# Another order for the 32 experts of a mixture-of-experts stage, and 64-row gathers for its half blocks

## The chip, the cores and the metric

The kernel runs on one core of one Trainium2 chip. The metric is the device time of one execution in microseconds (us); of several runs the median counts. Engines are named as in the profile: PE is TensorE (PEld its weight loads), DVE is VectorE, ACT is ScalarE, POOL is GpSimd, SP is SyncE, which here issues the large loads.

## The reference

One decoder layer with 2048 tokens of width 1024 in float32: projections, an RWKV-7 mixer and a dilated attention, an output product with layer norm, and then the part that the change touches, a mixture of 32 experts (two for each token), added to a gated embedding term, with a last layer norm. The expert part, cut:

```python
eid = grp[:, None] * EXPERTS_PER_GROUP + top_i          # two experts for each token
...
def run_block(args):                                    # 128 rows of one expert
    xblk, e = args
    hdn = jax.nn.silu(xblk @ w_gate[e]) * (xblk @ w_up[e])
    return hdn @ w_down[e]
...
return jnp.zeros((N, D), x2.dtype).at[row_tok].add((yb * row_w[:, None]).astype(x2.dtype))
```

`w_gate` and `w_up` are 1024 x 512 for each expert and `w_down` is 512 x 1024, so an expert has 6.3 MB of weights whatever the number of its tokens.

## The kernel before

The layer runs in stages: project, mixers, mix_out, route, ple (the gated embedding), experts, finish. The change touches the experts stage.

**Sizes and order.** The experts are sorted on the chip by how many tokens they got. `RANKS` (line 35) holds, for each place in that sorting, a size in units of 64 rows: one expert of 7, one of 5, one of 4, ten of 3, thirteen of 2 and six of 1. An expert of size n has n // 2 full blocks of 128 rows and, where n is odd, one half block of 64. `_order` (lines 39 to 48) fixes in which order the ranks are worked: it picks at each step the rank that keeps the sum of `UNITS` closest to its mean. `ORDER` and `CAPS` (sizes in that order) come from it. Before the change `CAPS` is 2,3 eight times, and then 2,2,3,2,3,2,4,2,1,5,1,1,1,7,1,1. Below, "a 3" is an expert of size 3.

**Groups.** `experts_begin` cuts each expert into groups of at most two blocks (line 1654). A 2 or a 1 is one group of one block; a 3 is one group of a full and a half block, a 4 one group of two full blocks; a 5 is a group of two full blocks and a group of one half block; a 7 is a group of two full blocks and one of a full and a half block.

**Work of a block.** float32 values are split into a high part (`copy` to fp32r on ACT) and a low part (subtraction on DVE), and a product is a sum of products of parts. A full block takes three matmuls of 512 columns for each 128 rows of weights (lines 198 to 200, `mm3`). A half block lays the high and low parts of its 64 rows beside each other in one operand and takes two (lines 1755, 1756); its two row halves have to be added afterwards (`sums`, lines 1768, 1769, and lines 1836, 1837). For each block the stage runs: `turn` (4+4 transposes of the gathered rows `xg` on PE, line 1746, then the parts `XX` on ACT and DVE, lines 1748, 1749), `pe_gate` (16 or 24 matmuls, then silu into `hd` on ACT, line 1789), `pe_up` (as many, then `hd` times it on DVE, line 1804), `pe_turn` (four transposes of `hd`, line 1812, then `HX` on ACT and DVE, lines 1813, 1814), `pe_down` (16 or 24 matmuls, then `ysb`), and a scatter that adds `ysb` to the result rows (line 1840, on POOL's queue).

**Weights.** Each expert has 12 pieces of 512 KB. SP loads them into 8 buffers (`raw`, `fetch`, line 1659), and `split` (line 1705) makes `wh` on ACT (line 1710) and `wl` on DVE (line 1711), two instructions of 512 columns each, into 12 buffers. `need` (line 1715) issues the splits at most six pieces (`LEAD`) ahead of the product.

**Order on the engines.** PE and ACT run in the order of the code; for the other engines a scheduler chooses. How a group of one block is joined to the next group matters below:

```python
more = turn(i + 1)
along(pe_up(i, 0), more)
...                                       # a group of two blocks does its products here, and pe_gate(i + 1) last
    along(pe_gate(i + 1), nothing, 3, lambda: pe_turn(i, 0))
run(pe_down(i, 0))
```

So after a one-block group PE runs the first three quarters of the next group's gate product, then the four transposes of `hd`, then the last quarter of that gate product, and then the down product, which needs `HX`.

**Gathers.** `gather(i)` (lines 1675 to 1680) fetches the rows of a group's blocks by an indirect DMA on POOL's queue, two groups ahead, into two buffers `xg`, always 128 rows; rows past the count of a block go to rows that are not used. `ix`, `sl` and `wd` are tables of row numbers and weights, loaded by POOL (lines 1641 to 1649) over the range of places that have such a block.

Of the kernel before, what the change touches and what calls it, by code (L numbers as in the profile page):

```python
# [18 lines left out]
P = 128  # L19
# [7 lines left out]
NE = 32  # L27
# [7 lines left out]
RANKS = (7, 5, 4) + (3,) * 10 + (2,) * 13 + (1,) * 6  # L35
UNITS = {n: n // 2 * 3 + n % 2 * 2 for n in range(33)}


def _order():

    left, done, order = list(range(NE)), 0, []
    mean = sum(UNITS[RANKS[r]] for r in left) / NE
    for n in range(NE):
        r = min(left, key=lambda r: (abs(done + UNITS[RANKS[r]] - AHEAD - mean * (n + 1)), r))
        left.remove(r)
        order.append(r)
        done += UNITS[RANKS[r]]
    return tuple(order)


AHEAD = 0.0
ORDER = _order()
CAPS = tuple(RANKS[r] for r in ORDER)
NW, NR, NX, NXX, NHX, NHD = 12, 8, 2, 4, 2, 2
# [113 lines left out]
class K:  # L168
# [1462 lines left out]
    def experts_begin(self):  # L1631

        nc, tc, I = self.nc, self.tc, self.I
        cp, rp = self.early
        lists = self.slots_[0:NE * CAP].rearrange("(e b p) w -> p e b w", b=CAP // P, p=P)
        nblk = (max(CAPS) + 1) // 2
        sl = cp.tile([P, NE, nblk, 2], F32, name="sl")
        ix = cp.tile([P, NE, nblk], I32, name="ix")
        wd = cp.tile([P, NE, nblk], F32, name="wd")
        for b in range(nblk):  # L1640
            js = [e for e in range(NE) if CAPS[e] > 2 * b]
            lo, hi = min(js), max(js) + 1
            nc.gpsimd.dma_start(sl[:, lo:hi, b], lists[:, lo:hi, b])
            nc.gpsimd.tensor_copy(ix[:, lo:hi, b], sl[:, lo:hi, b, 0])
            js = [e for e in range(NE) if CAPS[e] == 2 * b + 1]
            if js:
                lo, hi = min(js), max(js) + 1
                for h in range(2):
                    nc.gpsimd.dma_start(wd[h * 64:(h + 1) * 64, lo:hi, b:b + 1], lists[0:64, lo:hi, b, 1:2])
        self.lists = sl, ix, wd  # L1650
        groups = []
        for e in range(NE):
            blocks = [(e, b, CAPS[e] == 2 * b + 1) for b in range((CAPS[e] + 1) // 2)]
            groups += [(e, blocks[j:j + 2], j + 2 >= len(blocks)) for j in range(0, len(blocks), 2)]

        self.groups = groups
        self.raws, self.xgs, issued = {}, {}, []

        def fetch(g):

            e, n = divmod(g, NCH)
            if n == 0:
                at = tc.issue_after(issued[-NCH].ins) if len(issued) >= NCH else ExitStack()
                with at:
                    self.who = nc.values_load(self.ord[0:1, e:e + 1], engines=[mybir.EngineType.SP], min_val=0, max_val=NE - 1)
            self.raws[g] = raw = rp.tile([P, D], F32, name="raw5", tag="raw5")
            if n < 8:
                src = I["w_gate" if n < 4 else "w_up"][0].rearrange("e (k p) f -> p (e k) f", p=P)
                ins = nc.sync.dma_start(raw.rearrange("p (k f) -> p k f", k=2), src[:, bass.ds(self.who * KC + n % 4 * 2, 2)])
            else:  # L1670
                src = I["w_down"][0].rearrange("e d f -> (e d) f")
                ins = nc.sync.dma_start(raw, src[bass.ds(self.who * DE + (n - 8) * P, P)])
            issued.append(ins)

        def gather(i):
            if i >= len(groups):
                return
            for e, b, half in groups[i][1]:
                self.xgs[e, b] = xg = cp.tile([P, D], F32, name="xg", tag="xg", bufs=NX)
                nc.gpsimd.indirect_dma_start(out=xg, out_offset=None, in_=self.x2, in_offset=bass.IndirectOffsetOnAxis(ap=ix[:, e, b:b + 1], axis=0))  # L1680

        self.fetch, self.gather = fetch, gather
        self.ln2 = [self.rows_to(cp, n, I[n][0]) for n in ("ln2_g", "ln2_b")]
        for g in range(NR):
            fetch(g)
        gather(0)

    def experts(self):
# [307 lines left out]
```

## Time and profile before

| | us |
|---|---|
| median of 3 runs | 3246.5 (3241.99 to 3250.48) |
| profiled execution, its own time | 3253.92 |
| span of the profiled execution | 3252.1 |
| of it the expert products on PE, 2315.7 to 3171.5 | 855.8 |
| PE busy over the span | 2928.5 (90%) |
| DVE, ACT, POOL busy | 2113.1, 1526.9, 675.3 |

The profile is one execution taken by the hardware profiler. A busy PE is modelled from pipelined matmuls. In a line of the trace's timeline, the bracket at the end is how long the engine stood idle before the instruction, and what released it. The granted clock of PE is a share of 2.4 GHz.

### The profile page before, as it was taken

What the parts mean: (1) busy time and instruction counts of PE and PEld (TensorE: products, weight loads), DVE (VectorE), ACT (ScalarE), POOL (GpSimd) and SP (SyncE); (2) the same over time, 40 slices, a digit from 0 to 9 for tenths busy, and PEclk for the clock granted to TensorE, in tenths of its full rate; (3) what the DMA queues carried; (4) which work ended last, traced back from release to release, by engine and by line L of the source; (5) the groups of instructions that cost most, each with busy time, mean ns of one, the idle gap of its engine ahead of it and who ended that gap; (6) DMA issues with size and microseconds to landing.
All of it is one profiled execution on the core that took longest, in us unless ns stands there. A gap on an engine that the chain in (4) does not pass through costs nothing. (4 is left out here: it accounts for less than half of the span.)

```text
span 3252.1 us, 49914 instructions
## 1 busy us (share of the span) xinstructions
PE 2928.5 (90%) x17038; PEld 2335.2 (72%) x17039; DVE 2113.1 (65%) x4730; ACT 1526.9 (47%) x3650; POOL 675.3 (21%) x682
## 2 busy tenths in 40 slices
PE   8989888999798998998997899899999999998880
PEld 6666777777687777777786677788777777776560
DVE  4997333686564755666657678653587787766756
ACT  3444211555454544544444233311477777765642
POOL 0442000244100312112102122223011111112216
PEclk9999989999799889988898899999999999999885
DMA  5212433688725335235205453243499999987845
GB/s 166 80 56 95 103 88 80 203 273 266 154 60 123 100 79 132 69 76 139 65 22 144 138 177 123 96 140 94 175 307 323 324 304 322 313 295 225 289 130 210
DMA packets 364064, 533.09 MB, mean 164 GB/s; under 512 B 92376, under 2 KB 204640, under 8 KB 363792
## 3 DMA queue, kind: packets, MB, share of 16 engines
q1 hardware_dynamic: 330144, 459.09, 44.4%
q0 software_dynamic: 14496, 45.93, 6.0%
q10 hardware_dynamic: 19168, 24.86, 3.1%
q8 instruction: 136, 2.23, 0.3%
q14 instruction: 120, 0.98, 0.1%
HBM read 402.27 MB, written 128.06 MB: 163 GB/s over the span
## 5 line engine op out<-in xcount | busy, mean ns | idle before, releaser
L1711 DVE TENSOR_TENSOR wl<-raw,wh 128x512 fp32r<-128x512 f32 x768 | 478.0, 681 | 88.5 <-ACT wh L1710 87.9
L1710 ACT CAST wh<-raw 128x512 fp32r<-128x512 f32 x768 | 417.5, 620 | 12.2 <-DMA raw<-in_w_up_dram 10.5
L198 PE MATMUL ps<-xh,wh 128*128 128x512 f32 x640 | 263.1, 411 | 0.3 <-ACT xh L322 0.3
L199 PE MATMUL ps<-xl,wh 128*128 128x512 f32 x640 | 259.2, 405 | 0.9 <-DVE xl L323 0.8
L200 PE MATMUL ps<-xh,wl 128*128 128x512 f32 x640 | 257.9, 403 | 0.0
L1088 ACT ACTIVATE pe<-pe,ms 128x256 f32<-128x256 f32 (+1 forms) x384 | 174.9, 457 | 161.0 <-DVE ms L1085 153.3
L1840 POOL DMA_INDIRECT acc<-ysb,ix x48 | 96.5, 2010 | 623.0 <-ACT ysb L1839 402.6
L198 PE MATMUL pe<-wh,XX 128*128 128x512 f32 x480 | 199.3, 415 | 3.8 <-ACT wh L1710 3.8
L199 PE MATMUL pe<-wl,XX 128*128 128x512 f32 x480 | 191.8, 400 | 2.6 <-DVE wl L1711 2.6
L200 PE MATMUL pe<-wh,XX 128*128 128x512 f32 x480 | 190.7, 397 | 0.0
L198 PEld LDWEIGHTS ps<-xh,wh 128*128 128x128 f32 x640 | 125.1, 195 | 34.2 <-issue 2.8
L199 PEld LDWEIGHTS ps<-xl,wh 128*128 128x128 f32 x640 | 124.7, 195 | 29.9 <-DVE xl L323 2.3
L200 PEld LDWEIGHTS ps<-xh,wl 128*128 128x128 f32 x640 | 124.5, 194 | 29.6
L1094 PE MATMUL pl<-eye,pe 128*128 128x128 f32 x600 | 128.6, 307 | 10.1 <-ACT pe L1088 9.5
L1069 PE MATMUL pl<-KK,Q 128*128 128x256 f32 x432 | 116.4, 395 | 20.3 <-DMA KK<-ks 8.2
L1108 PE MATMUL po<-pe,V 128*64 128x128 f32 x1200 | 123.0, 309 | 8.6 <-DVE O L1122 7.0
L198 PE MATMUL pb<-gh,XH 128*128 128x512 f32 x320 | 126.0, 394 | 0.0
L199 PE MATMUL pb<-gl,XH 128*128 128x512 f32 x320 | 125.2, 391 | 0.0
L1755 PE MATMUL pe<-wh,XX 128*128 128x512 f32 x288 | 120.1, 417 | 5.4 <-ACT wh L1710 5.4
L200 PE MATMUL pb<-gh,XL 128*128 128x512 f32 x320 | 124.8, 390 | 0.0
L1756 PE MATMUL pe<-wl,XX 128*128 128x512 f32 x288 | 118.4, 411 | 3.0 <-DVE wl L1711 3.0
L198 PE MATMUL pa<-woh,YH 128*128 128x512 f32 x256 | 112.5, 439 | 3.1 <-ACT YH L1338 3.1
(418 smaller groups left out, 7565.2 us busy)
## 6 DMA issues: line engine op xcount, KB each, us to landing
raw<-in_w_gate_dram SPq DMA_DIRECT2D x128, 512.0 KB
raw<-in_w_up_dram SPq DMA_DIRECT2D x128, 512.0 KB
raw<-in_w_down_dram SPq DMA_DIRECT2D x128, 512.0 KB
pk<-pk SPq DMA_DIRECT2D x32, 512.0 KB
pk_t<-pk SPq DMA_DIRECT2D x32, 512.0 KB
KK<-ks SPq DMA_DIRECT2D x64, 256.0 KB
wr<-in_w_in_dram SPq DMA_DIRECT2D x48, 256.0 KB
rkk<-rkk SPq DMA_DIRECT2D x32, 384.0 KB
```

What stands on the lines that cost most here:

```text
L198: mm(out, lh, rh, start=first, stop=False)
L199: mm(out, lh, rl, start=False, stop=False)
L200: mm(out, ll, rh, start=False, stop=last)
L1069: mm(pl[:, h], q, toks(KK[:, m, h], n, prev, 2), start=m == 0, stop=m == 1)
L1088: nc.scalar.activation(pe[:, h, w], pe[:, h, w], AF.Exp, bias=m_[h], scale=-1.0, accum_out=s_[h])
L1094: nc.tensor.transpose(pt[:, h, b], pe[:, h, b * P:(b + 1) * P], self.c("eye"))
L1108: mm(o[h * 64:(h + 1) * 64, j], vb[:, h * 64:(h + 1) * 64], tt[:, h, b], start=b == kb[0], stop=b == 1)
L1710: nc.scalar.copy(wh[:, c], raw[:, c])
L1711: nc.vector.tensor_tensor(out=wl[:, c], in0=raw[:, c], in1=wh.bitcast(F32)[:, c], op=ALU.subtract)
L1755: mm(ps, L[:, 0:P], wh, start=first, stop=False)
L1756: mm(ps, L[:, 0:P], wl, start=False, stop=last)
L1840: nc.gpsimd.indirect_dma_start(out=self.acc, out_offset=bass.IndirectOffsetOnAxis(ap=ix[0:r, e, b:b + 1], axis=0), in_=ysb[0:r], in_offset ...
```

## The change

`_order` is written anew. The ranks of one size are spread evenly over 0 to 1 (of m ranks the i-th at (2i+1)/2m); the sizes that occur once go to rank/4 + 0.25, so the 7 to 0.25, the 5 to 0.5 and the 4 to 0.75. The order is the sorting by these places. `CAPS` becomes 2,3,1,2,3,2,7,3,1,2,2,3,1,2,3,5,2,3,2,1,3,2,2,4,3,1,2,3,2,1,3,2. And the gather of a half block fetches 64 rows.

```diff
 def _order():
 
-    left, done, order = list(range(NE)), 0, []
-    mean = sum(UNITS[RANKS[r]] for r in left) / NE
-    for n in range(NE):
-        r = min(left, key=lambda r: (abs(done + UNITS[RANKS[r]] - AHEAD - mean * (n + 1)), r))
-        left.remove(r)
-        order.append(r)
-        done += UNITS[RANKS[r]]
-    return tuple(order)
-
-
-AHEAD = 0.0
+    place = {}
+    for n in set(RANKS):
+        rs = [r for r in range(NE) if RANKS[r] == n]
+        for i, r in enumerate(rs):
+            place[r] = (2 * i + 1) / (2 * len(rs)) if len(rs) > 1 else r / 4 + 0.25
+    return tuple(sorted(range(NE), key=lambda r: (place[r], r)))
...
             for e, b, half in groups[i][1]:
                 self.xgs[e, b] = xg = cp.tile([P, D], F32, name="xg", tag="xg", bufs=NX)
-                nc.gpsimd.indirect_dma_start(out=xg, out_offset=None, in_=self.x2, in_offset=bass.IndirectOffsetOnAxis(ap=ix[:, e, b:b + 1], axis=0))
+                r = 64 if half else P
+                nc.gpsimd.indirect_dma_start(out=xg[0:r], out_offset=None, in_=self.x2, in_offset=bass.IndirectOffsetOnAxis(ap=ix[0:r, e, b:b + 1], axis=0))
```

In the changed kernel the same lines of code stand 2 or 3 lines earlier (1812 becomes 1810, 198 becomes 195, 1755 becomes 1753). PE runs the same instructions in another order. First, PE before, at a 2 that is followed by a 3: from the transposes of `hd` to the first matmul that needs `HX`.

```order
L1812 MATMUL tp_22883<-eye,hd 128x128 x4
L198 MATMUL pe_22792<-wh_22804,XX 128x512
L199 MATMUL pe_22792<-wl_22805,XX 128x512
L200 MATMUL pe_22792<-wh_22804,XX 128x512
L1755 MATMUL pe_22793<-wh_22804,XX 128x512
L1756 MATMUL pe_22793<-wl_22805,XX 128x512
L198 MATMUL pe_22792<-wh_22804,XX 128x512
L199 MATMUL pe_22792<-wl_22805,XX 128x512
L200 MATMUL pe_22792<-wh_22804,XX 128x512
L1755 MATMUL pe_22793<-wh_22804,XX 128x512
L1756 MATMUL pe_22793<-wl_22805,XX 128x512
L198 MATMUL pe_22907<-wh_22674,HX 128x512
```

Ten matmuls of the next gate product stand between the two. PE before, at the 27th expert, a 1 that is followed by a 1:

```order
L1812 MATMUL tp_29115<-eye,hd 128x64 x4
L1755 MATMUL pe_29043<-wh_29054,XX 128x512
L1756 MATMUL pe_29043<-wl_29055,XX 128x512
L1755 MATMUL pe_29043<-wh_29054,XX 128x512
L1756 MATMUL pe_29043<-wl_29055,XX 128x512
L1755 MATMUL pe_29131<-wh_28962,HX 128x512
```

Here four stand between them. PE in the changed kernel, at the third expert, a 1 that is followed by a 2:

```order
L1810 MATMUL tp_22845<-eye,hd 128x64 x4
L195 MATMUL pe_22767<-wh_22778,XX 128x512
L196 MATMUL pe_22767<-wl_22779,XX 128x512
L197 MATMUL pe_22767<-wh_22778,XX 128x512
L195 MATMUL pe_22767<-wh_22778,XX 128x512
L196 MATMUL pe_22767<-wl_22779,XX 128x512
L197 MATMUL pe_22767<-wh_22778,XX 128x512
L1753 MATMUL pe_22860<-wh_22668,HX 128x512
```

This join, with six matmuls of a full block's gate after a half block, does not occur in the kernel before; in the changed one it occurs four times. POOL before, at the loads of the tables that come ahead of the first gather:

```order
L1643 DMA sl<-slotlist 128x32x2
L1649 DMA wd<-slotlist 64x8x1 x2
L1643 DMA sl<-slotlist 128x29x2
L1649 DMA wd<-slotlist 64x20x1 x2
L1643 DMA sl<-slotlist 128x5x2
```

And POOL at the same place in the changed kernel:

```order
L1640 DMA sl<-slotlist 128x32x2
L1646 DMA wd<-slotlist 64x28x1 x2
L1640 DMA sl<-slotlist 128x30x2
L1646 DMA wd<-slotlist 64x30x1 x2
L1640 DMA sl<-slotlist 128x10x2
```

The loads cover longer ranges of places, since the half blocks and the large experts lie further apart in the new order. Eighteen of the 48 gathers that follow have 64 rows now.

## Rows read from the trace of the kernel before

**Rows 1.** The page: busy tenths of each engine, 40 slices of 81 us.
```profile
PE   8989888999798998998997899899999999998880
PEclk9999989999799889988898899999999999999885
DMA  5212433688725335235205453243499999987845
```

**Rows 2.** Stretches of the expert stage: width, then engines' busy time (instructions), clock.
```profile
core 0: us, PE busy (x) PEld busy (x) DVE busy (x) ACT busy (x) POOL busy (x), PEclk, DMA share, GB/s
2315.70:2377.20 61.50, 55.12 (x238) 43.21 (x237) 46.80 (x78) 43.62 (x82) 7.37 (x6) 0.92 0.85 299
2377.20:2720.40 343.20, 343.20 (x1598) 273.30 (x1596) 269.04 (x448) 253.92 (x477) 58.83 (x42) 1.00 0.94 317
2720.40:2791.90 71.50, 68.15 (x313) 53.42 (x312) 55.27 (x92) 52.16 (x99) 11.13 (x8) 1.00 0.95 322
2791.90:2894.90 103.00, 103.00 (x481) 83.11 (x480) 76.53 (x126) 72.20 (x135) 16.85 (x12) 1.00 0.93 306
2894.90:2924.00 29.10, 25.12 (x101) 19.18 (x100) 19.81 (x33) 19.23 (x37) 2.69 (x2) 0.88 0.93 306
2924.00:2947.80 23.80, 21.63 (x101) 16.60 (x101) 18.46 (x31) 17.77 (x35) 3.75 (x3) 1.00 0.90 312
2947.80:2997.40 49.60, 44.30 (x189) 33.75 (x188) 22.93 (x39) 22.59 (x43) 9.80 (x5) 0.93 0.63 184
2997.40:3021.90 24.50, 17.71 (x61) 11.39 (x61) 18.64 (x32) 16.78 (x33) 5.65 (x2) 0.79 0.81 287
3021.90:3046.40 24.50, 17.06 (x61) 11.37 (x60) 18.72 (x32) 16.82 (x33) 5.64 (x2) 0.79 0.82 287
3046.40:3070.50 24.10, 21.60 (x101) 16.57 (x101) 19.78 (x33) 18.06 (x35) 6.67 (x3) 1.00 0.83 292
3070.50:3126.70 56.20, 55.24 (x257) 43.76 (x257) 22.68 (x38) 22.84 (x43) 11.38 (x6) 1.00 0.48 137
3126.70:3155.30 28.60, 21.16 (x78) 14.57 (x76) 21.74 (x37) 19.90 (x39) 1.42 (x1) 0.82 0.73 235
3155.30:3171.50 16.20, 11.04 (x37) 8.12 (x35) 7.92 (x13) 6.54 (x13) 5.83 (x1) 0.79 0.13 17
```

**Rows 3.** Timeline of PE, instructions that waited: start, us, what [idle before, releaser].
```profile
2740.41 0.50 PE L198 MATMUL pe<-wh,HX 128*128 128x512 f32 x1 [1.75 <-ACT HX L1813]
2742.05 0.50 PE L200 MATMUL pe<-wh,HX 128*128 128x512 f32 x1 [0.91 <-DVE HX L1814]
...
2915.63 0.80 PE L198 MATMUL pe<-wh,HX 128*128 128x512 f32 x1 [3.98 <-ACT HX L1813]
...
2991.05 0.79 PE L1755 MATMUL pe<-wh,HX 128*128 128x512 f32 x1 [4.65 <-DVE HX L1814]
...
3003.97 0.49 PE L1755 MATMUL pe<-wh,XX 128*128 128x512 f32 x1 [1.46 <-ACT wh L1710]
3005.44 0.50 PE L1756 MATMUL pe<-wl,XX 128*128 128x512 f32 x1 [0.97 <-DVE wl L1711]
...
3016.01 0.79 PE L1755 MATMUL pe<-wh,HX 128*128 128x512 f32 x1 [3.50 <-DVE HX L1814]
```

**Rows 4.** Waits of ACT from 2330 to 3175: us in total, times, longest.
```profile
ACT wh L1710 <- DMA raw<-in_w_up_dram: 10.5, 12, 2.6
```

**Rows 5.** Timeline of POOL around the first gathers.
```profile
2233.49 1.78 POOL L1643 DMA_DIRECT2D sl<-slotlist  x1 [1.95 <-DMA slotlist<-pay,dest]
2235.26 1.43 POOL L1649 DMA_DIRECT2D wd<-slotlist  x2
2236.65 1.70 POOL L1643 DMA_DIRECT2D sl<-slotlist  x1
2238.33 1.81 POOL L1649 DMA_DIRECT2D wd<-slotlist  x2
2240.11 0.90 POOL L1643 DMA_DIRECT2D sl<-slotlist  x1
...
2247.24 1.03 POOL L1680 DMA_INDIRECT xg<-x,ix  x1 [0.65 <-POOL ix L1644]
2248.57 0.96 POOL L1680 DMA_INDIRECT xg<-x,ix  x1 [0.31 <-issue]
2317.49 0.95 POOL L1680 DMA_INDIRECT xg<-x,ix  x1 [67.96 <-PE tp L1746]
```

## The prediction

> **What bounds the kernel now.** I read the page's slices first [rows 1]: PE is busy in nine tenths of nearly every slice of the last third, and the DMA engines are full there too, so the expert stage could hang on either. The table by stretches decides [rows 2]. I cut the stage where a down product ends. Its second stretch is seven pairs of a 2 and a 3 (the pattern 2,3 from the third to the sixteenth expert): 343.2 us wide, PE busy 343.2 us, at full clock, with a DMA share of 0.94. There PE waits for nothing, and 1598 of its instructions take 343.2 us, 0.2148 us each. That is the price of PE's work, and PE's work does not change. Everything above it in another stretch is loss. Width minus count times 0.2148, row by row:
>
> - first two experts, with the start: 61.5 - 238 x 0.2148 = 10.4
> - 2,2,3: 71.5 - 313 x 0.2148 = 4.3; 2,3,2,4: -0.3
> - a 2 before a 1: 29.1 - 101 x 0.2148 = 7.4
> - a 1 before the 5: 23.8 - 21.7 = 2.1
> - the 5 before a 1: 49.6 - 40.6 = 9.0
> - a 1 before a 1, twice: 24.5 - 61 x 0.2148 = 11.4 each
> - a 1 before the 7: 24.1 - 21.7 = 2.4; the 7 itself 1.0
> - after the 7, a 1 before a 1: 28.6 - 16.8 = 11.8
> - the last 1: 16.2 - 7.9 = 8.3
>
> These sum to 79.2 us of 855.8. The loss sits at joins where a one-block group is followed by a one-block group ("narrow joins"): there are six, a 2 before a 2 (4.3), a 2 before a 1, the 5 before a 1 (its last group is one half block) and three times a 1 before a 1. A group of two blocks on either side costs nothing, or 2.1 to 2.4 after a 1. The timeline says why [rows 3]: the first down matmul stands idle for `HX`, 1.75 and 0.91 us in the 2 before a 2, 3.98 in the 2 before a 1, 4.65 after the 5, 3.50 in the 1 before a 1, where PE also waits 1.46 and 0.97 us for `wh` and `wl`. `HX` comes from `hd` through ACT and DVE, whose queues also hold the splits of the weights, and the order on PE puts ten gate matmuls in front of it where a 3 follows, six where a 2 follows and four where a 1 follows.
>
> **The change part by part.** *The order.* Of its 31 joins the new one has nine narrow ones: a 1 before a 2 four times, a 2 before a 2 twice, a 2 before a 1 twice, the 5 before a 2 once. A 1 stands before a 3 twice. Eight times a 2 stands before a 3, the 7 or the 4 (no loss, as in the seven pairs), and twelve times a two-block group comes first (no loss). So the rows of 1s go, but each 1 now meets a 2. The prices: a 2 before a 2 is 4.3 (twice 8.6), a 2 before a 1 is 7.4 (twice 14.8), a 1 before a two-block group 2.3 (twice 4.6).
>
> The 1 before a 2 is not in the trace of before. Its bounds are the 2 before a 2, 4.3, which has the same six matmuls of cover, and the 1 before a 1, 11.4, which has the same half block in front. I take it from the nearer of the two. The half block has the longer chain (its two row halves are added before silu, before the product with `hd`, and at the end), and it is this that ACT and DVE have to get through: in the 1-before-1 stretch DVE alone is busy 18.6 us against 61 x 0.2148 = 13.1 us of PE's work [rows 2]. A full gate in place of a half one gives PE eight more matmuls to run meanwhile, 8 x 0.2148 = 1.7 us, so 11.4 - 1.7 = 9.7 us, four times 38.8. The 5 before a 2 likewise: 9.0 - 1.7 = 7.3, bounds 4.3 and 9.0. The stage now ends with a 2 in place of a 1: between 0 and 8.3; I take 4.3, as for a full block whose chain is not covered. The first two experts are the same, 10.4.
>
> The sum: 10.4 + 8.6 + 14.8 + 4.6 + 38.8 + 7.3 + 4.3 = 88.8 us, 9.6 more than 79.2.
>
> *The clock.* The narrow joins before a 1 show a granted clock of 0.88, 0.93 and 0.79, so part of each stretch ran at 1.2 GHz and not 2.4; the stretch with the 2 before a 2 shows 1.00 with 2.7 us of idle time in it [rows 2, 3]. The prices above include what the clock cost. The Trainium skill (TensorE: Matmul & The Clock Gate, Part 1) says that the clock is binary, half after idling and full again after sustained work, and that the monitor runs freely, so the same code is hit in one run and not in another. By this rule the two joins of a 2 before a 2 could each pay what the 2 before a 1 paid, 0.12 x 29.1 = 3.5 us, and the sum would be 7 us higher; by the row it is not, and I take the row.
>
> *The gathers.* 18 gathers lose 64 rows of 4 KB, 0.26 MB each, 4.7 MB in all. At the 317 GB/s and the share of 0.94 of the seven pairs (337 GB/s when full) that is 0.78 us of transfer each, 14 us in all. It is beside PE's work in the pairs, where PE waits for nothing. What shows a wait for weights is 10.5 us of ACT in twelve waits [rows 4], and ACT is itself only part of the chain. I take 0; the bounds are 0 and -10.5. It would be worth more if another work no longer hid the transfers: the work that hides them is PE's.
>
> *The tables.* POOL's loads of `sl` and `wd` cover more places. Taken as growing with them, the 1.43 us issue pair (8 to 28) becomes 5.0, the 1.81 pair 2.7, and 0.90 becomes 1.8: 5.4 us later for the first gather, which is out at 2248.6, while POOL then stands idle for 68 us until PE turns its rows [rows 5]. Hidden; 5.4 us if that cover were gone. POOL's scatters queue behind the gathers as before. The last scatter has 128 rows for 64: under 1 us.
>
> Against the profiled execution this gives 3253.9 + 9.6 = 3263.5. The median of the runs shown is 7.4 below that execution, so the forecast is 3246.5 + 9.6, about **3256**.
>
> **The rivals.** The total as a function of the price p of a 1 before a 2 is 50.0 + 4p, so the change breaks even at p = 7.3, and it shows as a gain of over 0.3% (9.7 us, about what a measurement of this kernel can tell from no change) below p = 4.9.
>
> *Faster: the 1s were dear because they stood in a row.* Their weights come at 287 GB/s with a DMA share of 0.81, and ACT waits for them [rows 2, 4]; a row of 1s uses up the eight raw and twelve split buffers, where a single 1 behind a 3 finds its pieces loaded. Then p is that of the 2 before a 2, and so is the 5 before a 2: 88.8 - 4 x 5.4 - 3.0 = 64.2, that is 15 us less than before, 3231.5. Against it: in the 1-before-1 row the long idle time ends with `HX`, not with a weight; six pieces of look-ahead are half an expert; and 10.5 us of waits for loads are few beside 79.
>
> *Slower by more: the lag is handed on.* After a 1 the queues of ACT and DVE are late, and the 2 behind it pays again at its own join with a 3 (2.3 us, four times), both joins of a 2 before a 2 fall into the half clock (7 us), and the end costs 8.3 as before: 9.2 + 7 + 4 = 20 us more, 3276. For it speaks that the 1 before the 5 and the 7, wide joins, cost 2.1 and 2.4 at full clock; against it that the 2,2,3 stretch as a whole cost 4.3.
>
> *The gathers pay on the path.* The full 10.5 us come off the waits, and the order's loss is cancelled: 3245.5. The Trainium skill (DMA: Bandwidth & Descriptors, Rules for kernel authors) says that DMAs issued from SP, ACT and GpSimd run on the same 16 engines and interleave, so by this rule fewer gathered rows bring the weights in sooner. The trace's 0.94 share with PE never idle says that sooner need not matter.
>
> **How the numbers follow.** The forecast has 0.55, and its own range is 3246 to 3266 (p from 7.2 to 11.4, the clock). Faster has 0.13, slower by more 0.15, the paying gathers 0.17. Slower by over 0.3%, above 3256.2: about half of the forecast's weight, 0.30, and 0.15, so 0.45. Faster by over 0.3%, below 3236.8: 0.13. Within: 0.25 + 0.17 = 0.42. The range leaves out most of the first rival and the far end of the second: 3237 to 3273.
>
> **What would show it.** In the profile after, the stretches that hold 2,3 pairs should keep 0.2148 us for each PE instruction. At each of the four places with a 1 before a 2 the down matmul of line 1753 should stand idle for `HX` by 2 to 4 us, and the loss should be 8 to 11 us; near 4 the first rival holds. Waits of ACT for `raw` should nearly vanish, which alone would prove nothing. If idle time appears at a 2 before a 3, the lag is handed on. The forecast is wrong in kind if a stretch with two-block groups, say around the 7, loses time, since I gave it none.

## The result: 0.84% slower, and the rows that answer to those of before

The changed kernel takes 3277.2 us in the median of six runs, the kernel before 3246.2 us beside it (one of its six executions took 8884.1 us, the other five lie between 3241.9 and 3250.5). The ratio on record is 1.0084, 95% interval 1.0062 to 1.0106, which is some 27 us; the two medians stand 31 us apart. I had forecast 3256, a range up to 3273, and 9.6 us of loss; the direction is right, the size is not.

| profiled execution | span | product stage begins | its width | behind it |
|---|---|---|---|---|
| before | 3252.1 | 2315.7 | 855.4 | 81.0 |
| before, again | 3250.9 | 2312.8 | 856.7 | 81.3 |
| changed | 3278.1 | 2321.7 | 874.3 | 82.1 |
| changed, again | 3253.4 | 2300.9 | 870.6 | 81.9 |
| changed, third time | 3274.4 | 2312.7 | 879.8 | 81.9 |

(us; the width is from the first transpose of `xg` to the start of the last down matmul.) The tail is the same within 1.1 us. Where the stage begins is scatter: in twelve profiles of this study, whose code up to there differs in a few table loads at most, it lies between 2299.9 and 2321.7, without regard to the order. What the change moves is the stage: 14 to 24 us more.

The page's slices of the changed kernel, PE, its clock and the DMA engines:

```profile
PE   8989888999798998998997899899999899999990
PEclk9999999999898888888997999999999999999995
DMA  5213433788625335235206353243596897998976
```

Where [rows 1] end in 8880 for PE and in 7845 for the DMA engines, these end in 9990 and 8976: the bad corner at the end of the stage is gone, and the loss lies elsewhere. The table by stretches says where it lies now, cut where a down product ends: a 1 before a 2, the 2 before a 3 behind it, another 1 before a 2, a 2 before a 2 (behind a 1), the 5 before a 2, a 2 before a 1, a 1 before a 3, a 2 before a 2 (behind a 3), the last 2.

```profile
core 0: us, PE busy (x) PEld busy (x) DVE busy (x) ACT busy (x) POOL busy (x), PEclk, DMA share, GB/s
2382.90:2411.70 28.80, 22.13 (x85) 16.68 (x84) 21.67 (x36) 19.64 (x38) 2.78 (x2) 0.88 0.96 312
2411.70:2436.30 24.60, 23.52 (x109) 18.04 (x108) 19.59 (x33) 18.23 (x35) 6.75 (x3) 1.00 0.83 296
2671.20:2698.40 27.20, 21.70 (x85) 16.45 (x84) 21.67 (x36) 19.64 (x38) 2.40 (x2) 0.87 1.02 323
2602.40:2626.40 24.00, 20.68 (x86) 15.72 (x85) 18.24 (x30) 16.34 (x31) 5.66 (x2) 0.93 0.83 270
2745.10:2804.90 59.80, 55.66 (x246) 43.67 (x245) 25.48 (x42) 25.58 (x48) 6.51 (x5) 0.97 0.63 176
2850.10:2878.00 27.90, 23.88 (x101) 18.18 (x100) 21.02 (x35) 19.30 (x37) 2.53 (x2) 0.94 1.02 314
2878.00:2901.20 23.20, 21.20 (x93) 15.88 (x92) 18.61 (x32) 18.12 (x36) 3.58 (x3) 0.93 0.90 308
2922.10:2948.90 26.80, 24.14 (x110) 19.05 (x109) 20.86 (x34) 19.10 (x36) 2.76 (x2) 1.00 0.98 336
3176.80:3196.20 19.40, 17.89 (x77) 13.60 (x75) 10.09 (x16) 8.94 (x17) 3.65 (x1) 1.00 0.24 38
```

One correction to how I read [rows 2]: an instruction that lies across a cut is counted in both stretches, so a row's count is one or two too high. Counted once, the stage has 3600 PE instructions before and after, and the seven pairs of before have 1596, at 343.2 / 1596 = 0.2150 us. By that the first row above lost 28.8 - 84 x 0.2150 = 10.7 us, the second 24.6 - 108 x 0.2150 = 1.4. The loss of the whole stage is 81.5 us before (82.8 in its second profile; I had read 79.2) and 100.4, 96.7 and 105.9 in the three profiles of the changed kernel. "Loss" below is counted so. It is of two kinds. In the first row PE's busy time is 22.13 us, so of the 10.7 us some 6.7 are idle time and 4.1 are matmuls at the lower clock, with a granted clock of 0.88 in the stretch.

### The profile page after: what moved, and what is told of

Its sections match the earlier page's. It is cut to its first block, busy times and chain, and to the rows that moved or that the text cites. A ratio compares the mean times of both kernels' runs of the same rounds, so it can differ in the third digit from the quotient of the medians.

```text
span 3278.1 us, 49906 instructions
## 1 busy us (share of the span) xinstructions
PE 2942.6 (90%) x17038; PEld 2341.9 (71%) x17039; DVE 2116.7 (65%) x4730; ACT 1526.4 (47%) x3650; POOL 676.0 (21%) x682
## 5 line engine op out<-in xcount | busy, mean ns | idle before, releaser
L1708 ACT CAST wh<-raw 128x512 fp32r<-128x512 f32 x768 | 417.4, 622 | 19.7 <-DMA raw<-in_w_up_dram 18.3
L195 PE MATMUL pe<-wh,XX 128*128 128x512 f32 x480 | 205.5, 428 | 17.1 <-ACT wh L1708 17.1
L196 PE MATMUL pe<-wl,XX 128*128 128x512 f32 x480 | 198.3, 413 | 6.0 <-DVE wl L1709 5.9
L197 PE MATMUL pe<-wh,XX 128*128 128x512 f32 x480 | 195.2, 407 | 0.0
L195 PEld LDWEIGHTS pe<-wh,XX 128*128 128x128 f32 x480 | 94.2, 196 | 41.0 <-ACT wh L1708 19.6
L1082 DVE CUSTOM_DVE_ANT_0 pe<-pl,bias 128x256 f32<-128x256 f32 x216 | 82.7, 419 | 54.8 <-PE pl L1066 37.6
L1753 PE MATMUL pe<-wh,XX 128*128 128x512 f32 x288 | 117.7, 409 | 0.0
```

The costliest lines, as they stand in the source:

```text
L195: mm(out, lh, rh, start=first, stop=False)
L196: mm(out, lh, rl, start=False, stop=False)
L197: mm(out, ll, rh, start=False, stop=last)
L1082: nc.vector.tensor_tensor_reduce(out=pe[:, h, w], in0=pl[:, h, w], in1=add[:, h, w], scale=1.0, scalar=3e38, op0=ALU.add, op1=ALU.min, acc ...
L1708: nc.scalar.copy(wh[:, c], raw[:, c])
L1753: mm(ps, L[:, 0:P], wh, start=first, stop=False)
```

## The experiments

The first four ran together, on one chip.

**The gathers alone.** The order of before, with only the second hunk of the change.

> The order of before, with the 64-row gathers of the change. My prediction gave the gathers 0, with bounds 0 and -10.5 us. If that is right, the expert stage keeps 855 us within 2 and the time is that of before within 3 us (3246). If the gathers pay on the path, the stage loses up to 10.5 us (845, time 3236). A third case: shorter gathers disturb the weight loads no less and the half blocks' turn comes earlier, worth 1 to 2 us in each row of 1s.

Measured: 3250.2 against 3248.5, ratio 1.0005 (0.9989 to 1.0021). The stage takes 853.6 us against 855.4 and 856.7. ACT's waits for `raw` are 10.5 us as in [rows 4]. The gathers are worth 2 to 3 us of stage at most, and nothing that the runs can tell.

**The order alone.** The new order with the old gather, `out=xg` and 128 rows.

> The new order, with 128-row gathers as before. If the gathers are worth nothing, the stage takes 874.7 us as in the changed kernel and the time is 3277 within 5. If the shorter gathers gave something back in the changed kernel, this one is slower by up to 10 us, most of it at the four places where a 1 stands before a 2.

Measured: 3279.6, ratio 1.0092 (1.0068 to 1.0116), stage 879.6. That lies in the scatter of the changed kernel's own profiles (870.6 to 879.8). So the result is the order's, as far as the runs can tell.

**Every 1 between groups of two blocks.** Only the order differs from the changed kernel:

```diff
-    place = {}
...
-    return tuple(sorted(range(NE), key=lambda r: (place[r], r)))
+    caps = (2, 3, 1, 3, 2, 2, 7, 1, 3, 2, 2, 3, 1, 3, 2, 2, 5, 3, 1, 3, 2, 2, 4, 1, 3, 2, 2, 3, 1, 3, 2, 2)
+    left = list(range(NE))
+    order = []
+    for n in caps:
+        r = min(r for r in left if RANKS[r] == n)
+        left.remove(r)
+        order.append(r)
+    return tuple(order)
```

> The changed kernel with another order: 2,3,1,3,2,2,7,1,3,2,2,3,1,3,2,2,5,3,1,3,2,2,4,1,3,2,2,3,1,3,2,2, in which every 1 stands between groups of two blocks, and the narrow joins are six of a 2 before a 2. By the theory of joins (loss sits where a one-block group meets a one-block group): start 10.4, six 1s before a two-block group at 3.65, five 2-before-2 at 4.5, the last one with the end 6.6, the 5 before a 3 at 3.4, 2.4 for the rest, together 67 us against 81.5 before (counted with each instruction once): stage 841, time 3232. By the rival theory of feeding (a 1 costs about 11 us wherever it stands, since its weights take as long as those of a 2: in before the 2,1,5 costs 9.9, the row of three 1s 35, the last two 20.5; in the changed kernel 3,1,2,3 costs 11 to 13): 10.4 + 66 + 29 + 3.4 = 109 us, stage 883, time 3274. A wait of PE for wh at the first gate matmul after a 1 tells which.

Measured: 3242.0, ratio 0.9983 (0.9964 to 1.0002), stage 853.5, loss 79.6. Neither number came. The theory of feeding falls by its price: a 1 cost 4.2 to 5.5 us, not 11, and PE waited for no `wh` behind it. (It waited for `XX` there instead, 2.5 to 2.9 us, see below.) But my prices fell too. First the stretch of a 1 before a 3, then that of a 2 before a 2:

```profile
2361.80:2389.60 27.80, 24.85 (x109) 18.88 (x108) 23.01 (x39) 21.40 (x42) 3.53 (x3) 0.94 1.02 341
2410.50:2437.30 26.80, 24.14 (x109) 19.04 (x108) 20.85 (x34) 18.98 (x36) 2.79 (x2) 1.00 1.00 338
```

and PE's timeline in the first of them:

```profile
2372.25 0.46 PE L1746 MATMUL tp<-eye,xg 64*128 64x64 f32 x4 [2.92 <-DVE XX L1749]
```

At these joins PE waits in the turn of the next group, since the `XX` of a transpose stands among the splits on ACT and DVE, as `HX` does. And the 2 before a 2 cost 5.1 to 6.3 us in five places out of six, not 3.6. So a join has no fixed price; as I read it, it depends on how late ACT and DVE come into it.

**The changed kernel again, twice, and before again.**

> The changed kernel once more. The stage took 874.7 us in its profile against 855.8 before, 18.9 more, and begins at 2321.7 instead of 2315.7. If these 6 us ahead of the stage are scatter between executions, the start lies anywhere from 2312 to 2325 here and the time is near 3268; if they belong to the change (the longer table loads of POOL), the start is again 2321 or more. The stage should repeat within 2 us.

Measured: 3275.1, ratio 1.0089 (1.0063 to 1.0114). The profiled execution began the stage at 2300.9, twenty us earlier than the first, so the lateness ahead of the stage was scatter. The stage did not repeat within 2 us: 870.6 against 874.3. The last two runs, together on one chip, followed that up:

> The kernel before, profiled a second time. The product stage should repeat 855 us within 2. The stage began anywhere from 2299.9 to 2321.7 in nine profiles whose code ahead of it is the same but for some table loads; if that is scatter, this one begins there too, and 2315.7 of the first profile was late by some 7 us.

> The changed kernel, profiled a third time, against before on the same chip. Open is a difference: the medians stand 25 to 31 us apart, the product stages of the profiles only 15 to 19, the tail 0.7. If the rest is scatter ahead of the stage, more runs bring the medians to 18 to 22 apart. If the changed kernel's stage itself scatters upwards (more of its nine narrow joins at the half clock than in the two profiles so far), this stage takes 875 to 882.

Measured: before 3249.7, ratio to itself 0.9997 (0.9978 to 1.0017), stage 856.7. The changed kernel 3276.2, ratio 1.0062 (1.0035 to 1.0089), stage 879.8. These two profiles begin the stage within 0.2 us of each other, and their spans differ by 3274.4 - 3250.9 = 23.5 us, which is the stage's 879.8 - 856.7 = 23.1 but for the tail. And the changed kernel's stage does scatter upwards. The same two stretches of it in this third profile, the 2 before a 2 behind a 3 and the 5 before a 2, which had 26.80 us at a clock of 1.00 and 59.80 at 0.97:

```profile
2915.90:2944.10 28.20, 25.54 (x109) 20.08 (x108) 20.86 (x34) 18.92 (x36) 2.76 (x2) 0.94 0.96 322
2736.80:2797.90 61.10, 56.96 (x245) 44.64 (x244) 25.48 (x42) 25.55 (x48) 6.51 (x5) 0.94 0.62 172
```

Width less PE's busy time is the same, 26.80 - 24.14 = 28.20 - 25.54 = 2.66 us, and 59.80 - 55.66 = 61.10 - 56.96 = 4.14 us. DVE and ACT did the same work. Only PE's clock was lower, for a longer part of the stretch: behind the wait for `HX`, matmuls stand 0.42 to 0.43 us apart (the 1.2 GHz level) six times in place of none, and twelve times in place of five. That cost 1.4 and 1.3 us. The kernel before has the same scatter. Its 2 before a 2 lost 3.6 us in the first profile and 5.2 in the second, again with 2.67 us of width less busy time:

```profile
2717.40:2745.80 28.40, 25.73 (x110) 20.16 (x109) 20.86 (x34) 19.05 (x36) 3.02 (x2) 0.94 0.97 319
```

**What fills the queue in front of `HX`.** The timelines of the changed kernel at its first 1 before a 2. PE:

```profile
2394.64 0.51 PE L195 MATMUL pe<-wh,XX 128*128 128x512 f32 x1 [3.22 <-ACT wh L1708]
2395.80 0.50 PE L196 MATMUL pe<-wl,XX 128*128 128x512 f32 x1 [0.66 <-DVE wl L1709]
...
2401.51 0.46 PE L1810 MATMUL tp<-eye,hd 64*128 64x64 f32 x4
...
2406.36 0.50 PE L1753 MATMUL pe<-wh,HX 128*128 128x512 f32 x1 [2.79 <-DVE HX L1812]
```

ACT and DVE at the same time:

```profile
2396.65 6.34 ACT L1708 CAST wh<-raw 128x512 fp32r<-128x512 f32 x12
2403.02 0.37 ACT L1811 CAST HX<-tp 128x256 fp32r<-128x256 f32 x1
```
```profile
2400.47 5.49 DVE L1709 TENSOR_TENSOR wl<-raw,wh 128x512 fp32r<-128x512 f32 x9
2405.89 0.41 DVE L1812 TENSOR_TENSOR HX<-tp,HX 128x256 fp32r<-128x256 f32 x1
```

The transposes of `hd` start at 2401.5, but their cast stands behind twelve casts of weights and its subtraction behind nine, and the down matmul starts at 2406.4. The twelve come from `need`: behind a one-block group the code asks for the next expert's gate pieces ahead of this expert's down pieces, so the number of the piece asked for jumps by five at the join, and the look-ahead with it. The same jump stands in the steady pairs, where the gate product of a 3 has 40 matmuls to cover it. That ACT and DVE take their work strictly in the order of the queue is also what the Trainium skill says (Perfetto Trace Analysis, Tensor Engine Instruction (MATMUL, LD_WEIGHTS)); the rows agree.

The edit takes the jump out. No instruction is added or dropped; the splits of the gate behind a one-block group run three pieces less ahead, and the down product issues them:

```diff
-            def need(g):
+            def need(g, back=0):
-                while done[0] < min(g + 1 + min(LEAD, g // 2 + 1), NP) and (done[0] <= g or done[0] < done[2] + NW):
+                while done[0] < min(g + 1 + min(LEAD, g // 2 + 1) - back, NP) and (done[0] <= g or done[0] < done[2] + NW):
...
-                        need(e * NCH + k // 2)
+                        need(e * NCH + k // 2, back)
...
-                        need(e * NCH + 8 + k)
+                        need(e * NCH + 8 + k + ahead)
...
-                        along(pe_gate(i + 1), nothing, 3, lambda: pe_turn(i, 0))
+                        along(pe_gate(i + 1, 3), nothing, 3, lambda: pe_turn(i, 0))
...
-                    run(pe_down(i, 0))
+                    run(pe_down(i, 0, 4 if i + 1 < len(groups) else 0))
```

It was made on the changed kernel, on the one before, and on the order with every 1 apart; beside them the changed kernel with the transposes of `hd` earlier (`nothing, 2, lambda: pe_turn(i, 0)`), which gives the down product more matmuls of cover and leaves the queue as it is (twelve casts and nine subtractions stand in front of `HX` there too).

> The changed kernel with the weight splits held back at the joins: in the gate product behind a one-block group the splits run three pieces less ahead, and the down product behind it issues them instead. No instruction is added; 4 pieces in place of 6 stand between the products of a 1 and its HX on ACT and DVE. If the HX wait is the queue of splits in front of it (in the changed kernel 12 casts, 6.3 us, stand there on ACT and nine subtractions, 5.5 us, on DVE), each of the nine narrow joins loses some 2 to 4 us less: HX waits of PE fall from 26 us to under 10, stage 845 to 855, time 3245 to 3260. If instead ACT and DVE, or the loads, are the rate (the same number of splits has to be through before the next products), the wait only moves from HX to wh and wl of the following products, stage 870 or more, time 3272.

> The kernel before with the same holding back. By the queue theory its six narrow joins lose 2 to 4 us less each: stage 855.6 - 18 = 838, time 3230. By the rate theory the rows of 1s go on losing 11 us for each 1, stage 852 or more.

> The order in which every 1 stands between two-block groups, with the same holding back. It lost 79.6 us: 9.8 at the start, 29 in six 1s before a 3, 31 in six 2-before-2 joins, 3 at the end. By the queue theory the 2-before-2 joins fall to 2 us and the stage to 835, time 3225. By the rate theory it stays at 854, time 3242. The 1s before a 3 wait for XX of the turn (2.9 us each), not for HX, and shouldn't move by either.

> The changed kernel with the transposes of hd after half of the next gate product in place of three quarters: 12 matmuls of a 2 in front of the down product, not 6. If what is missing at a join is matmuls between the transposes and the down product (the cover of my prediction), each narrow join gains up to 6 x 0.215 = 1.3 us, stage 863. If the queue in front of HX sets the time, the transposes' place changes nothing, because HX's cast stands behind the same casts: stage 872 to 876; the transposes may even wait for hd.

| kernel | median us | ratio to before (95%) | stage us | loss us |
|---|---|---|---|---|
| changed, splits held back | 3213.7 | 0.9883 (0.9858 to 0.9908) | 824.1 | 50.1 |
| before, splits held back | 3217.9 | 0.9902 (0.9877 to 0.9928) | 823.0 | 49.1 |
| 1s apart, splits held back | 3211.3 | 0.9881 (0.9855 to 0.9907) | 820.5 | 46.6 |
| changed, transposes earlier | 3276.8 | 1.0064 (1.0044 to 1.0085) | 880.0 | 106.1 |

The cover falls: with six more matmuls in front of the down product nothing is gained. The queue stands, and with more than I expected of it: the changed kernel loses 50 us less, the one before 32 less. In the order with the 1s apart each 2 before a 2 falls from 3.6 to 6.3 us to 1.2, and the 1s before a 3 keep their loss, 4.3 to 5.7 us after 4.2 to 5.5, with 2.5 to 2.9 us of waiting for `XX`, as expected. The whole stage, first in the changed kernel, then with the splits held back:

```profile
2321.70:3196.00 874.30, 813.05 (x3600) 631.95 (x3599) 618.71 (x1034) 579.32 (x1092) 147.91 (x93) 0.96 0.84 272
```
```profile
2307.00:3131.10 824.10, 792.83 (x3601) 623.25 (x3599) 621.03 (x1034) 581.31 (x1092) 131.04 (x93) 0.98 0.89 289
```

Of the 50 us, 30 are PE's idle time (874.3 - 813.1 = 61.2 against 31.3) and 20 its busy time for the same 3600 instructions, at a granted clock of 0.96 and of 0.98. In the changed kernel held back, the same join, ACT and DVE:

```profile
2381.99 4.26 ACT L1708 CAST wh<-raw 128x512 fp32r<-128x512 f32 x8
2387.35 0.37 ACT L1811 CAST HX<-tp 128x256 fp32r<-128x256 f32 x1 [1.10 <-PE tp L1810]
```
```profile
2385.81 3.08 DVE L1709 TENSOR_TENSOR wl<-raw,wh 128x512 fp32r<-128x512 f32 x5
2388.82 0.41 DVE L1812 TENSOR_TENSOR HX<-tp,HX 128x256 fp32r<-128x256 f32 x1
```

Eight casts and five subtractions in place of twelve and nine, and ACT now waits for PE there. What PE waits for from 2340 to 3190, first in the changed kernel, then with the splits held back (us in total, times, longest):

```profile
PE pe L195 <- ACT wh L1708: 14.8, 6, 3.2
PE pe L1753 <- DVE HX L1812: 12.7, 5, 4.1
PE tp L1744 <- DVE XX L1747: 10.7, 12, 2.0
PE pe L195 <- ACT HX L1811: 9.8, 5, 3.5
PE pe L196 <- DVE wl L1709: 5.9, 6, 2.2
PE pe L197 <- DVE HX L1812: 3.4, 8, 1.2
...
```
```profile
PE pe L195 <- ACT wh L1708: 12.9, 4, 3.2
PE pe L197 <- DVE HX L1812: 4.7, 4, 1.6
PE pe L1753 <- DVE HX L1812: 2.5, 3, 1.7
PE pe L196 <- DVE wl L1709: 2.1, 4, 0.7
PE tp L1744 <- DVE XX L1747: 1.1, 4, 0.3
...
PE pe L195 <- ACT HX L1811: 0.7, 1, 0.7
PE pe L1753 <- DVE XX L1747: 0.4, 2, 0.2
```

The waits for `HX` fall from 25.9 us to 7.9, those for `XX` from 10.7 to 1.5. The four waits for `wh`, one at each 1 before a 2, stay, 3.2 us each. They may be the rate theory's share, since a 1 gives PE 60 x 0.2150 = 12.9 us of work, and 24 casts and 24 subtractions, at 6.34 / 12 and 5.49 / 9 us as above, take ACT 12.7 and DVE 14.6 us. But shortly before such a wait (the matmul at 2379.98) ACT itself stands idle, for the sum `us`, which DVE has behind its own subtractions:

```profile
2375.62 0.63 ACT L1787 ACTIVATE hd<-us 64x512 f32<-64x512 f32 x1 [1.53 <-DVE us L1767]
```

So these waits can be a matter of order as well; no run tells which. And the two orders come out alike, 824.1 and 823.0 us of stage: what the change lost against before went with the splits in front of `HX`. The edit also shortens ACT's waits for loads (the last section), and no run takes that apart from the queue.

The three kernels with the splits held back are 1.0 to 1.2% faster than the kernel before, and so beat the changed one too. Between the three the runs don't decide.

## Why the prediction was wrong, by its steps

The rule that PE's work stays and only losses move held: both executions have 3600 instructions, and where wide joins follow one another nothing is lost (the 2 before the 7, behind a 3: -0.05 us; the 7 itself: -0.2). The terms, my price against the mean of the three profiles of the changed kernel:

| term | predicted | measured |
|---|---|---|
| start | 10.4 | 10.3 |
| four 1s before a 2 | 38.8 | 39.8 (9.1 to 9.2, or 10.7 to 10.8 each) |
| the 5 before a 2 | 7.3 | 7.8 |
| two 2s before a 2 | 8.6 | 10.4 |
| two 2s before a 1 | 14.8 | 13.7 |
| two 1s before a 3 | 4.6 | 7.3 |
| the last 2 | 4.3 | 3.0 |
| a 2 before a two-block group, behind a narrow join, six times | 0 | 7.5 |
| the rest | 0 | 1.3 |
| sum | 88.8 | 101.1 |
| before, on the same count | 79.2 | 82.2 |

Against before the change was to cost 9.6 us of stage; it cost 101.1 - 82.2 = 18.9.

The unknown on which I spent most thought, the 1 before a 2, came out: 9.7 predicted, 9.95 on average. That is luck in part. I had put it on the wait for `HX`, 2 to 4 us. The profiles show 1.6 to 2.8 us for `HX`, and ahead of it 3.2 us for `wh` and 0.4 to 0.7 for `wl`, which the prediction had only inside the price of a 1 before a 1 (1.46 and 0.97 us there). The 5 before a 2 was close, too. The gathers' 0 held, and the tables' loads show no loss. ACT's waits for `raw`, which I expected nearly to vanish, grew, from 10.5 and 8.7 us in the two profiles of before to 18.3, 14.1 and 14.0. Two steps failed.

**The wide join was priced at zero.** I took "a 2 before a 3 costs nothing" from seven pairs in which ACT and DVE are never late, and used it for places where they come out of a narrow join behind. There each 2 before a 3 lost 1.0 to 2.6 us (1.4 in the second row of the table by stretches), each 1 before a 3 lost 3.4 to 4.8 in place of 2.3: together 7.5 + 2.7 = 10 us of the 12.3 by which the sum was short (3.0 of the 12.3 are no loss of the change, since my count of before was as much too low). This is the rival "the lag is handed on", which gave 3276 and to which I gave 0.15. The trace had shown it: its 2,2,3 stretch holds a 2 before a 3 that lost 1.0 of the 4.3 us. I priced the whole stretch as one number, and so didn't ask what the 3 behind other narrow joins would lose. The rival's own parts are not all right: its 8.3 for the end was 3.0.

**The clock was read off one row.** I weighed 7 us for the two 2-before-2 joins, and took the row at 1.00 instead. The measured difference is smaller, 1.4 to 1.6 us for such a join, but the other narrow joins have it too: the 1 before a 2 costs 9.1 or 10.7, the 5 before a 2 7.3 or 8.7, the 2 before a 1 6.4 to 7.5, and the stage 870.6 to 879.8. The sentence of the Trainium skill that I cited (TensorE: Matmul & The Clock Gate, Part 1), by which the same code is hit in one run and not in another, is what the two executions show, though the page has it for the start of a kernel; I should have put that scatter into the range for nine joins in place of six. My forecast's upper end for its own case, 3266, had room for neither step.

What the stage explains of the measured time: its width grew by 14 to 24 us from profile to profile, 23.1 in the pair that began alike. The ratios, 1.0084, 1.0089 and 1.0062, are 20 to 29 us, each with an interval of 7 to 9 us to either side; the medians stand 26 to 31 us apart. Whether the executions that were timed and not profiled have more joins at the low clock, as the third profile has, or whether a few us lie elsewhere, no run here shows.

As for the cause, I was half right. I named `HX` and the queues of ACT and DVE, and explained the differences between joins by the matmuls of cover and the longer chain of a half block. The moved transposes show that more cover is worth nothing while the queue stands; holding back the splits takes 50 of the 100 us away, and 27 of the 37 us for which PE waits for `HX` and `XX`. I read the code of `need` as "six pieces ahead" and missed the jump.

## What to carry to other kernels

When an engine's queue is filled ahead by a look-ahead rule, follow the rule across the place where the consumer's order jumps: a burst of prefetch work lands there in front of the one short instruction on which everything waits, and here putting it behind cost nothing that the runs show. A price read from a steady stretch holds for a place only if the engines that feed it enter it as early as in that stretch; sum the losses behind a stall until they are zero, not to the end of the stall. Before a schedule is reordered to avoid dear joins, it is worth finding what makes them dear: here the order was worth 20 to 30 us one way, and the queue, by the medians, 35 us the other way in the old order (3252.7 and 3217.9, timed together) and some 60 in the new one (3275 to 3277 and 3213.7, not timed together).

## What the hardware showed that I had not expected

- The weights came in faster once the splits were spread: 289 GB/s over the stage in place of 272, for the same loads in a shorter stage. In the stretch of a 1 before a 3 (2878.0 above, 308 GB/s and a DMA share of 0.90) the kernel with the splits held back shows 377 GB/s and a share of 1.04:

```profile
2832.80:2853.30 20.50, 19.77 (x94) 14.99 (x93) 17.39 (x31) 16.61 (x33) 3.84 (x3) 1.00 1.04 377
```

- ACT's waits for `raw` nearly vanished with it, though the loads keep their order: first the changed kernel (14.1 and 14.0 us in its other profiles), then with the splits held back.

```profile
ACT wh L1708 <- DMA raw<-in_w_up_dram: 18.3, 12, 3.8
```
```profile
ACT wh L1708 <- DMA raw<-in_w_down_dram: 0.4, 1, 0.4
```

  Before and before with the splits held back show 10.5 [rows 4] and 2.0. So those waits were no bound of the loads as such; that the buffers had come free late is what I read from it, and was not tried by itself.
- The same instructions with the same idle time took 1.3 to 1.6 us longer in one execution than in another, by the granted clock alone (0.94 for 1.00 and for 0.97), and the stage of one kernel ranged over 9 us in three profiles; the kernel before repeated within 1.3 us in two.
